# A two-block network on one core: ALiBi bias built on VectorE, norm factors later, q and k of the first group read amid v, and the attentions' value products beside the next scores

## The chip, the cores and the metric

One core of a Trainium2 chip runs the whole program. Its engines run side by side: PE (matmuls; its weight loads are PEld), DVE (VectorE), ACT (ScalarE), POOL (GpSimd) and SP, which issues the DMAs. The metric is the device time of one execution in microseconds (us).

## The reference

The input is a sequence of 256 tokens of width 1024. Two blocks follow each other, each with two layers; all of it is in float32.

```
block 1, layer 0:  h += diff_attention(rmsnorm(h))         8 heads, two softmax maps each
   s = q k^T / 8 - slope[head] * |i - j|                   ALiBi bias
   o = (softmax(s_0) - lam * softmax(s_1)) v ; rmsnorm over each head's 128 ; @ w_o
block 1, layer 1:  h += neighborhood_attention(rmsnorm(h)) 16 heads, windowed bias ; @ w_o
after each of the two:
   h += (silu(n @ w_gate) * (n @ w_up)) @ w_down           n = rmsnorm(h), hidden 2816
   h += sigmoid(rmsnorm(h) @ w_gate_ple) * (p @ w_proj)    "PLE"
h = rmsnorm(h)                                             final norm of block 1
block 2, layer 0:  h += even_mixer(rmsnorm(h))   z = n @ w_in: gated causal convolution | pooling
block 2, layer 1:  h += odd_attention(rmsnorm(h))  8 forgetting heads and 8 block heads, causal
after each of the two: a gated FFN, hidden 2816, with a causal convolution
out = rmsnorm(h)
```

## The kernel before

**Layout.** Activations lie transposed: `h` has the 1024 features on 128 partitions by 8 tiles, and the 256 tokens in the free dimension. A product of weights and activations has 8 steps of k (128 features each). To keep float32 precision on fp32r matmuls each operand is split in a high and a low part, and a product is three matmuls: hi by hi, hi by lo and lo by hi (`mm3`, all at L220). One 128-by-256 output over k = 1024 thus takes 24 matmuls.

**Weights.** SP brings chunks of 512 KB into five stage buffers. `split()` (L96, L97) makes of each chunk `w_hi` on ACT and `w_lo` on DVE, into eight split buffers. Taking a chunk for use triggers the split of a later one, so DVE and ACT have one split to do for every chunk that PE consumes. `W.hold` keeps these splits back while a layer's end is evicted; `release()` and `pay()` let them go, one per tick.

**Order.** PE's order is written by hand. The other engines' orders are made by a scheduler from the program order. `tick()` counts steps: it runs after every 12 matmuls of a weight product. `at(delay, f)` sets a small job `f` (scores, transposes, value products, a norm's factors) at that many ticks later, into the stream of matmuls. The table `AT` has these delays for the three attentions: for two pairs of heads per group, the tick of the scores, and under "then" how long after them the transposes, the values and (da only) the transposes back come. "last" is the group that has no next one.

**Norms.** A norm's gain is multiplied in at once (`norm_bank`: `u_hi` on ACT L282, `u_lo` on DVE L284), its per-token factor later, when products leave PSUM. `stats_bank` sums squares (ACT, DVE L275). `rstd_a` adds the two halves (`half`, DVE L291), sums over partitions with four small matmuls (`ps_ss`), and takes the power -1/2: DVE L306, POOL L307. `rstd_b` spreads the factor with two transposes (`ps_r`, PE L323) and an ACT eviction to `R`. `rstd_soon(n, a, b)` sets `rstd_a` at tick a and `rstd_b` at tick b.

**First products of a layer.** `first_pairs` makes the first two pairs of outputs (four weight chunks) in two passes, so that PE can begin while the last tiles of `u` are still being made: first k = 0 to 5 of all four outputs, then k = 6 and 7. `late=2` is the number of k steps left for the second pass. The banks of `u` (two tiles each) come in order from the layer before.

**Group 0 of an attention** (`qkv_group`) makes the pairs of q and k, then ticks until `R` exists, evicts q and k with it (DVE; ACT L475 and DVE L476 make hi and lo parts), and only then begins v (`ps_v`, 48 matmuls).

**Start.** `small_constants`, at tick 9, makes the ALiBi bias: `dist` on DVE (L571), then eight 128-by-512 `bias` tiles on POOL (L573), the causal masks, and small scalars. POOL takes instructions in order, so the first norm's power at L307 stands behind the eight.

**Block 2, even mixer.** `scale_h` (L932) applies the final norm of block 1 to `h`: eight DVE instructions, at tick 8. The outputs of `w_in` are worked on by DVE alone (`pool_out`, `gc_val` with `z_ev` L972, `gate_b`). In the FFNs `gu` (L835) is the first read of a product, with `R`.

Of the kernel before, what the change touches and what calls it, by code (L numbers as in the profile page):

```python
# [18 lines left out]
S = 256  # L19
# [17 lines left out]
    "da": {"scores": (3, 9), "then": (6, 8, 12), "last": ((2, 5), (5, 7, 10)), 0: (6, 10)},  # L37
    "na": {"scores": (3, 9), "then": (6, 8), "last": ((2, 5), (5, 7)), 0: (6, 10)},
    "od": {"scores": (3, 9), "then": (6, 8), "last": ((2, 5), (5, 7)), 0: (12, 15), 1: (6, 9)},
# [84 lines left out]
def network(ctx: ExitStack, tc: tile.TileContext, x_t, p_t, cols, b_v, na_bias, t5_bias, w_mats, out):  # L124
# [90 lines left out]

    def col(name, i):
        return ct[:, COL[name] + i:COL[name] + i + 1]
# [116 lines left out]
    def rstd_soon(n, a=7, b=9):  # L334
        at(4, release)
        at(a, lambda: rstd_a(n))
        at(b, lambda: rstd_b(n))
# [130 lines left out]
    def qkv_group(n, g, kind, bv, steps):  # L468
# [12 lines left out]
        ps_k = None  # L481
        if g == 0 and kind != "da":
            ps, ps_k = first_pairs(u)
        else:
            ps = pair(u)
            if g == 0:
                ps_k = pair(u)
        while g == 0 and not hasattr(n, "R"):
            tick()
        if kind == "na":  # L490
            t = work.tile([128, 2, S], F32, tag="qb", bufs=1, name="qb")
            nc.vector.tensor_mul(t, ps, bc2(n.R))
            for i in range(2):
                nc.scalar.activation(q[:, i, :], t[:, i, :], AF.Identity, bias=b_q8[:, 2 * g + i:2 * g + i + 1],
                                     scale=0.125)
        else:
            nc.vector.scalar_tensor_tensor(q, ps, 0.125, bc2(n.R), op0=OP.mult, op1=OP.mult)
        q = parts(q, "q")
        ps = ps_k or pair(u)
        if kind == "na":  # L500
            t = work.tile([128, 2, S], F32, tag="qb", bufs=1, name="kb")
            nc.vector.tensor_mul(t, ps, bc2(n.R))
            for i in range(2):
                nc.scalar.activation(k[:, i, :], t[:, i, :], AF.Identity, bias=col("b_k", 2 * g + i), scale=1.0)
        else:
            nc.vector.tensor_mul(k, ps, bc2(n.R))
        k = parts(k, "k")
        steps(q, k, v)
        if kind == "od" and g == 0:
# [3 lines left out]
            for n_k in (3, 3, 2):  # L513
                hi, lo = W.take(n_k * 264)
                for i in range(n_k):
# [5 lines left out]
                    if kk % 2 == 0:  # L521
                        tick()
            for t in range(2):
# [6 lines left out]
        for half in range(2):  # L530
            hi, lo = W.take(1024)
            for i in range(4):
# [5 lines left out]
                if i % 2 == 1:  # L538
                    tick()
        for t in range(2):  # L540
# [29 lines left out]

# [638 lines left out]
```

## Time and profile before

| | |
|---|---|
| median of 3 runs | 1254.99 us (1249.63 to 1255.4) |
| the profiled execution | 1255.7 us, span in the trace 1253.9 us |
| PE busy | 1219.8 us, 97% of the span |
| DVE busy | 930.2 us, 74% |
| ACT busy | 693.4 us, 55% |
| POOL busy | 56.5 us, 5% |
| HBM traffic | 220 MB, 176 GB/s |

A busy share is an average over the whole program. PE does nearly all the time what only PE can do, so what there is to gain or lose lies in three things: the few times at which PE stands still, the clock that it is granted afterwards, and the pace at which equal matmuls follow each other.

### The profile page before, as it was taken

The numbers are of one execution on the slowest core, as the hardware profiler recorded it, in microseconds if no ns is written. First come the engines' busy times: TensorE is split into PE (matmuls) and PEld (weight loads), VectorE is DVE, ScalarE is ACT, GpSimd is POOL, SyncE is SP. The second block draws the span as 40 slices with busy tenths as digits, with TensorE's granted clock in tenths as the row PEclk, the third lists the DMA queues.
The fourth block names the chain that finished last, engine by engine and source line by source line (L and its number), as shares of the span: only waits on it lengthen the run. The fifth ranks groups of instructions, "written<-read, shape, count | busy, mean of one in ns | idle before, by whom it ended". The sixth has DMA issues, their size and how long they took to land.

```text
span 1253.9 us, 25715 instructions
## 1 busy us (share of the span) xinstructions
PE 1219.8 (97%) x10448; PEld 1199.9 (96%) x10448; DVE 930.2 (74%) x1700; ACT 693.4 (55%) x1178; POOL 56.5 (5%) x64
## 2 busy tenths in 40 slices
PE   4999999999999999999999999999999999999997
PEld 4999999999999899999998999999999899999996
DVE  5876766666888767666678978777787876977773
ACT  4776644444667655454457555555455665545543
POOL 6011000000001000000000000000000000000000
PEclk9999999999999999999999999999999999999998
DMA  7554556555557436555544465555545333655530
GB/s 265 186 169 152 174 202 203 196 194 168 202 174 204 175 135 211 193 202 195 180 157 160 160 227 183 200 188 186 185 154 203 122 131 135 218 185 185 187 117 35
DMA packets 62935, 222.46 MB, mean 177 GB/s; under 512 B 7264, under 2 KB 7776, under 8 KB 62688
## 3 DMA queue, kind: packets, MB, share of 16 engines
q1 hardware_dynamic: 60768, 214.52, 50.2%
q0 software_dynamic: 1616, 5.77, 1.9%
q8 instruction: 82, 1.34, 0.4%
q10 hardware_dynamic: 432, 0.53, 0.1%
q14 instruction: 37, 0.30, 0.1%
HBM read 219.74 MB, written 1.05 MB: 176 GB/s over the span
## 4 chain that ended last, share of the span: by engine, by line
PE 86%; DVE 6%; issue 3%; POOL 2%; ACT 2%; DMA 1%; POOLq 0%; DVEq 0%; ACTq 0%; SPq 0%
PE ps_g L220 50%; PE acc L220 26%; PE ps_v L220 4%; DVE w_lo L97 2%; PE ps_V L220 2%; POOL bias L573 1%; PE ps_S L220 1%; PE ps_t L433 1%; POOL rstd L307 1%; ACT w_hi L96 1%; PE ps_p L220 1%; ACT sc L463 0%; PE pz L220 0%; DMA stage<-w_ev_out 0%; PE ps_ss L220 0%
## 5 line engine op out<-in xcount | busy, mean ns | idle before, releaser
L96 ACT ACTIVATE w_hi<-stage 128x1024 fp32r<-128x1024 f32 (+2 forms) x413 | 426.6, 1040 | 411.4 <-PE ps_g L220 174.4
L97 DVE TENSOR_TENSOR w_lo<-stage,w_hi 128x1024 fp32r<-128x1024 f32 (+2 forms) x413 | 493.1, 1201 | 194.8 <-ACT w_hi L96 191.3
L220 PE MATMUL ps_g<-u_hi,w_hi 128*128 128x256 f32 x2048 | 576.5, 281 | 10.2 <-ACT w_hi L96 7.0
L220 PE MATMUL ps_g<-u_hi,w_lo 128*128 128x256 f32 x2048 | 571.1, 279 | 1.2 <-DVE w_lo L97 1.2
L220 PE MATMUL ps_g<-u_lo,w_hi 128*128 128x256 f32 x2048 | 571.3, 279 | 0.7 <-DVE u_lo L284 0.6
L220 PEld LDWEIGHTS ps_g<-u_hi,w_hi 128*128 128x128 f32 x2048 | 386.2, 189 | 14.5 <-ACT w_hi L96 7.0
L220 PEld LDWEIGHTS ps_g<-u_hi,w_lo 128*128 128x128 f32 x2048 | 386.3, 189 | 1.4 <-DVE w_lo L97 1.4
L220 PEld LDWEIGHTS ps_g<-u_lo,w_hi 128*128 128x128 f32 x2048 | 385.8, 188 | 1.1 <-DVE u_lo L284 1.1
L220 PE MATMUL acc<-m,w_hi 128*128 128x256 f32 x1408 | 246.5, 278 | 0.1
L220 PEld LDWEIGHTS acc<-m,w_hi 128*128 128x128 f32 x1408 | 213.6, 188 | 0.4 <-DVE m L805 0.3
L220 PE MATMUL acc<-m,w_lo 128*128 128x256 f32 x704 | 195.4, 278 | 0.0
L220 PEld LDWEIGHTS acc<-m,w_lo 128*128 128x128 f32 x704 | 132.2, 188 | 0.0
L220 PE MATMUL acc<-u_hi,w_hi 128*128 128x256 f32 x256 | 73.0, 285 | 0.0
L220 PE MATMUL acc<-u_hi,w_lo 128*128 128x256 f32 x256 | 71.4, 279 | 0.0
L220 PE MATMUL acc<-u_lo,w_hi 128*128 128x256 f32 x256 | 71.3, 279 | 0.0
L463 ACT ACTIVATE sc<-sc,st 128x256 f32<-128x256 f32 (+1 forms) x96 | 46.0, 481 | 31.4 <-DVE st L461 31.3
L307 POOL TENSOR_TENSOR rstd<-rstd,mhalf 128x2 f32<-128x2 f32 x11 | 15.7, 1426 | 1036.6 <-DVE rstd L306 1036.6
L220 PE MATMUL ps_v<-w_hi,u_hi 128*128 128x256 f32 x176 | 52.5, 298 | 0.0
L220 PE MATMUL ps_v<-w_hi,u_lo 128*128 128x256 f32 x176 | 50.3, 286 | 0.0
L220 PE MATMUL ps_v<-w_lo,u_hi 128*128 128x256 f32 x176 | 50.3, 286 | 0.0
L220 PEld LDWEIGHTS acc<-u_hi,w_hi 128*128 128x128 f32 x256 | 48.0, 188 | 1.5 <-issue 1.1
L220 PEld LDWEIGHTS acc<-u_hi,w_lo 128*128 128x128 f32 x256 | 48.1, 188 | 0.0
(191 smaller groups left out, 1226.8 us busy)
## 6 DMA issues: line engine op xcount, KB each, us to landing
stage<-w_gu SPq DMA_DIRECT2D x88, 512.0 KB, 4.2
stage<-w_in SPq DMA_DIRECT2D x88, 512.0 KB, 4.2
stage<-w_down SPq DMA_DIRECT2D x44, 512.0 KB, 4.3
stage<-w_out SPq DMA_DIRECT2D x44, 512.0 KB, 4.3
stage<-w_na_qkv SPq DMA_DIRECT2D x24, 512.0 KB, 4.2
stage<-w_da_qkv SPq DMA_DIRECT2D x23, 512.0 KB, 4.3
stage<-w_od_in SPq DMA_DIRECT2D x22, 512.0 KB, 3.5
stage<-w_gate SPq DMA_DIRECT2D x16, 512.0 KB, 3.2
```

The costliest lines, as they stand in the source:

```text
L96: self.nc.scalar.activation(hi[:, s], t[:, s], AF.Copy)
L97: self.nc.vector.tensor_sub(lo[:, s], t[:, s], hi[:, s].bitcast(F32))
L220: nc.tensor.matmul(o, a, b, start=start, stop=stop, **kw)
L307: nc.gpsimd.tensor_tensor(n.rstd, st[:, 2:4], mhalf, op=OP.pow)
L433: nc.tensor.transpose(ps[:, o:o + 128], a[:, qt, kk * 128:(kk + 1) * 128], ident)
L463: nc.scalar.activation(sc[:, i, :widths[i]], sc[:, i, :widths[i]], AF.Exp, bias=st[:, 2 + i:3 + i], accum_out=st[:, 4 + i:5 + i])
L573: nc.gpsimd.tensor_scalar(da_tiles[hd // 4][:, hd % 4], dist, -2.0 ** (-8.0 * (hd + 1) / 8), None, op0=OP.mult)
```

## The change

It has five parts. (1) The ALiBi bias moves from POOL to DVE. `dist`, the mask, the pooling counts and three of the eight bias tiles are made at the program's start, the fourth at tick 9 and the other four at tick 22; the second weight chunk is split in two halves. (2) `rstd_soon` spreads a norm's factor one tick later by default (10 for 9). After the FFNs of block 1 both of its steps come two ticks earlier (5 and 7); after the last PLE they are at 7 and 11, with `scale_h` at 13 for 8. (3) Group 0 of an attention no longer ticks until `R` is there: v begins right behind q and k, and q and k are evicted after the first tick of v at which `R` exists; the scores' delays for this group are shorter by one tick (od: two). (4) "then" sets the values at the tick (12) at which the next pair's transposes come, and da's transposes back at 18. (5) `first_pairs` gets `late=4` in na and in the even mixer, and PLE evicts its first two outputs before its third pair of products instead of after.

On DVE, at the program's start, these rows run from the first full-size split to the second split behind `half`, before (`w_lo` is a weight split, `ssq` and `half` are the first norm's sums):

```order
L97 TENSOR_TENSOR w_lo<-stage,w_hi 128x1024
L275 TENSOR_TENSOR ssq<-ssq,sq 128x512
L97 TENSOR_TENSOR w_lo<-stage,w_hi 128x1024 x2
L275 TENSOR_TENSOR ssq<-ssq,sq 128x512
L97 TENSOR_TENSOR w_lo<-stage,w_hi 128x1024
L275 TENSOR_TENSOR ssq<-ssq,sq 128x512
L577 RECIPROCAL rcnt<-rcnt 128x64
L97 TENSOR_TENSOR w_lo<-stage,w_hi 128x1024
L291 TENSOR_TENSOR half<-ssq 128x256
L578 TENSOR_SCALAR off<-off 128x256
L97 TENSOR_TENSOR w_lo<-stage,w_hi 128x1024
L306 TENSOR_SCALAR rstd<-ps_ss 128x2
```

and after, from the last quarter of the first chunk to the same `rstd`:

```order
L97 TENSOR_TENSOR w_lo<-stage,w_hi 128x256
L97 TENSOR_TENSOR w_lo<-stage,w_hi 128x512 x2
L97 TENSOR_TENSOR w_lo<-stage,w_hi 128x1024
L287 TENSOR_TENSOR ssq<-ssq,sq 128x512
L97 TENSOR_TENSOR w_lo<-stage,w_hi 128x1024
L287 TENSOR_TENSOR ssq<-ssq,sq 128x512
L97 TENSOR_TENSOR w_lo<-stage,w_hi 128x1024 x2
L287 TENSOR_TENSOR ssq<-ssq,sq 128x512
L97 TENSOR_TENSOR w_lo<-stage,w_hi 128x1024 x2
L303 TENSOR_TENSOR half<-ssq 128x256
L97 TENSOR_TENSOR w_lo<-stage,w_hi 128x1024
L318 TENSOR_SCALAR rstd<-ps_ss 128x2
```

`half` stood behind five full splits. It now stands behind six, behind the two half-size ones of the second chunk, and, further up, behind three of the `bias` rows. `rstd` follows one split later, as before.

On PE, in the second group of da, at the tick where one pair's scores are made, before (`ps_V` from `ident` are transposes back, `ps_t` transposes, `ps_S` scores, `ps_g` the weight product around them):

```order
L220 MATMUL ps_g<-u_hi,w_lo 128x256
L638 MATMUL ps_V<-ident,on 128x128 x2
L433 MATMUL ps_t<-ident,a 128x128 x4
L220 MATMUL ps_S<-k_hi,q_hi 128x256 x2
L220 MATMUL ps_S<-k_lo,q_hi 128x256 x2
L220 MATMUL ps_S<-k_hi,q_lo 128x256 x2
L220 MATMUL ps_S<-k_hi,q_hi 128x256 x2
L220 MATMUL ps_S<-k_lo,q_hi 128x256 x2
L220 MATMUL ps_S<-k_hi,q_lo 128x256 x2
L220 MATMUL ps_g<-u_hi,w_hi 128x256
```

and after:

```order
L232 MATMUL ps_g<-u_hi,w_lo 128x256
L653 MATMUL ps_V<-ident,on 128x128 x2
L232 MATMUL ps_V<-v,at 128x128 x4
L445 MATMUL ps_t<-ident,a 128x128 x4
L232 MATMUL ps_S<-k_hi,q_hi 128x256 x2
L232 MATMUL ps_S<-k_lo,q_hi 128x256 x2
L232 MATMUL ps_S<-k_hi,q_lo 128x256 x2
L232 MATMUL ps_S<-k_hi,q_hi 128x256 x2
L232 MATMUL ps_S<-k_lo,q_hi 128x256 x2
L232 MATMUL ps_S<-k_hi,q_lo 128x256 x2
L232 MATMUL ps_g<-u_hi,w_hi 128x256
L232 MATMUL ps_g<-u_lo,w_hi 128x256
```

The four value products of the earlier pair (`ps_V<-v,at`), which had their own place two ticks later, now stand in the same break of the weight stream, ahead of the transposes.

On PE at the end of da's last group, before:

```order
L220 MATMUL acc_1426<-u_lo,w_hi 128x256
L220 MATMUL acc_1426<-u_hi,w_lo 128x256
L638 MATMUL ps_V<-ident,on 128x128 x2
L220 MATMUL ps_V<-v,at 128x128 x4
L220 MATMUL acc_1427<-u_hi,w_hi 128x256
L220 MATMUL acc_1427<-u_lo,w_hi 128x256
```

and after:

```order
L232 MATMUL acc_1423<-u_lo,w_hi 128x256
L232 MATMUL acc_1423<-u_hi,w_lo 128x256
L653 MATMUL ps_V<-ident,on 128x128 x2
L232 MATMUL ps_V<-v,at 128x128 x8
L232 MATMUL acc_1424<-u_hi,w_hi 128x256
L232 MATMUL acc_1424<-u_lo,w_hi 128x256
```

Here the transposes back and two pairs' value products fall in one place: ten small matmuls in a row that need three tiles of PSUM tag "m", of which there are two.

```diff
@@ -34,9 +34,9 @@
 
 
 AT = {
-    "da": {"scores": (3, 9), "then": (6, 8, 12), "last": ((2, 5), (5, 7, 10)), 0: (6, 10)},
-    "na": {"scores": (3, 9), "then": (6, 8), "last": ((2, 5), (5, 7)), 0: (6, 10)},
-    "od": {"scores": (3, 9), "then": (6, 8), "last": ((2, 5), (5, 7)), 0: (12, 15), 1: (6, 9)},
+    "da": {"scores": (3, 9), "then": (6, 12, 18), "last": ((2, 5), (5, 7, 10)), 0: (5, 9)},
+    "na": {"scores": (3, 9), "then": (6, 12), "last": ((2, 5), (5, 7)), 0: (5, 9)},
+    "od": {"scores": (3, 9), "then": (6, 12), "last": ((2, 5), (5, 7)), 0: (10, 13), 1: (6, 9)},
 }
 
 
@@ -213,6 +213,18 @@
     causal = off
     tri = const.tile([128, 128], F32, name="tri")
 
+    def da_bias(heads):
+
+        for hd in heads:
+            nc.vector.tensor_scalar(da_tiles[hd // 4][:, hd % 4], dist, -2.0 ** (-8.0 * (hd + 1) / 8), None, op0=OP.mult)
+
+    nc.vector.tensor_scalar(tri, off[:, :128], 0.0, None, op0=OP.is_ge)
+    nc.vector.scalar_tensor_tensor(dist, dist, -1.0, dist, op0=OP.mult, op1=OP.max)
+    da_bias(range(3))
+    for g, w in enumerate(POOL_WINDOWS):
+        nc.vector.tensor_scalar(rcnt[:, g, :], rcnt[:, g, :], float(w), None, op0=OP.min)
+    nc.vector.reciprocal(rcnt, rcnt)
+
     def col(name, i):
         return ct[:, COL[name] + i:COL[name] + i + 1]
 
@@ -331,7 +343,7 @@
     def release():
         W.hold = False
 
-    def rstd_soon(n, a=7, b=9):
+    def rstd_soon(n, a=7, b=10):
         at(4, release)
         at(a, lambda: rstd_a(n))
         at(b, lambda: rstd_b(n))
@@ -478,34 +490,40 @@
 
...
-        ps_k = None
-        if g == 0 and kind != "da":
-            ps, ps_k = first_pairs(u)
+        def evict_q(ps):
...
+            else:
+                nc.vector.scalar_tensor_tensor(q, ps, 0.125, bc2(n.R), op0=OP.mult, op1=OP.mult)
+            return parts(q, "q")
+
+        def evict_k(ps):
...
+            else:
+                nc.vector.tensor_mul(k, ps, bc2(n.R))
+            return parts(k, "k")
+
+        waiting = []
+        if g:
+            qs = evict_q(pair(u))
+            steps(qs, evict_k(pair(u)), v)
         else:
-            ps = pair(u)
-            if g == 0:
-                ps_k = pair(u)
-        while g == 0 and not hasattr(n, "R"):
-            tick()
...
-        ps = ps_k or pair(u)
...
-        k = parts(k, "k")
-        steps(q, k, v)
+            waiting += first_pairs(u, late=4 if kind == "na" else 2) if kind != "da" else [pair(u), pair(u)]
+
+        def read():
+            if waiting and hasattr(n, "R"):
+                qs = evict_q(waiting[0])
+                steps(qs, evict_k(waiting[1]), v)
+                waiting.clear()
+
         if kind == "od" and g == 0:
             z = small.tile([128, 2, 8], F32, tag="zf", bufs=1, name="zf")
             pz = [psum.tile([128, 264], F32, tag=f"acc{2 + t}", name="pz") for t in range(2)]
@@ -520,6 +538,8 @@
                     kk += 1
                     if kk % 2 == 0:
                         tick()
+                        read()
+            assert not waiting
             for t in range(2):
                 nc.scalar.activation(v[:, t, :], pz[t][:, :256], AF.Copy, scale=n.rstd[:, t:t + 1])
                 nc.vector.scalar_tensor_tensor(z[:, t, :], pz[t][:, 256:264], n.rstd[:, t:t + 1],
@@ -537,6 +557,8 @@
                            kk == 0 and t == 0 and c == 0, kk == 7 and c == 2, skip_group_check=True)
                 if i % 2 == 1:
                     tick()
+                    read()
+        assert not waiting
         for t in range(2):
             if kind == "na":
                 nc.vector.scalar_tensor_tensor(v[:, t, :], pv[:, t, :], n.rstd[:, t:t + 1], bv,
@@ -567,14 +589,7 @@
     g_fm = const.tile([128, 8], F32, name="g_fm")
 
     def small_constants():
-
-        nc.vector.scalar_tensor_tensor(dist, dist, -1.0, dist, op0=OP.mult, op1=OP.max)
-        for hd in range(8):
-            nc.gpsimd.tensor_scalar(da_tiles[hd // 4][:, hd % 4], dist, -2.0 ** (-8.0 * (hd + 1) / 8), None, op0=OP.mult)
-        nc.vector.tensor_scalar(tri, off[:, :128], 0.0, None, op0=OP.is_ge)
-        for g, w in enumerate(POOL_WINDOWS):
-            nc.vector.tensor_scalar(rcnt[:, g, :], rcnt[:, g, :], float(w), None, op0=OP.min)
-        nc.vector.reciprocal(rcnt, rcnt)
+        da_bias([3])
         nc.vector.tensor_scalar(causal, off, 128.0, NEG, op0=OP.is_gt, op1=OP.mult)
         l = COL["lam"]
         pr = work.tile([128, 2, 64], F32, tag="dump", bufs=1, name="pr")
@@ -874,12 +889,12 @@
         for b in range(4):
             if b == 0:
                 pgs = first_pairs(n.u, between=proj)
+                continue
+            if b == 1:
                 held = [(i, pps[i], pgs[i]) for i in range(2)]
-            elif b > 1:
+            else:
                 proj(b)
                 held.append((b, pps[b], pair(n.u, *(("m", 2) if b == 2 else ("g", 2)))))
-            if b < 2:
-                continue
             for i, pp, pg in held:
                 z = work.tile([128, 2, S], F32, tag="a", bufs=3, name="z")
                 nc.vector.tensor_mul(z, pg, bc2(n.R))
@@ -899,13 +914,14 @@
 
     n = Norm()
     W.split(4, lambda b: norm_bank(n, b, h[:, 2 * b:2 * b + 2, :], lambda t: col("norm_mix", t)))
-    W.split()
+    W.split(2)
     for b in range(4):
         stats_bank(n, b, h[:, 2 * b:2 * b + 2, :])
         W.split()
     for _ in range(N_HI - 8):
         W.split()
     at(9, small_constants)
+    at(22, lambda: da_bias(range(4, 8)))
     ug = [const.tile([128, 2 + S], F32, name=f"ug{i}") for i in range(3)]
     for t in ug:
         nc.gpsimd.memset(t[:, 0:2], 0.0)
@@ -914,7 +930,7 @@
     for l in range(2):
         n = attention(n, ("da", "na")[l], lambda t, l=l: col("norm_ffn", 8 * l + t))
         n = ffn(n, swiglu_mid, lambda t, l=l: col("norm_ple", 8 * l + t))
-        rstd_soon(n)
+        rstd_soon(n, 5, 7)
         if l == 0:
             def after(nn):
                 rstd_soon(nn)
@@ -932,8 +948,8 @@
             nc.vector.scalar_tensor_tensor(h[:, t, :], h[:, t, :], col("norm_final", t), r,
                                            op0=OP.mult, op1=OP.mult)
 
-    rstd_soon(n)
-    at(8, scale_h)
+    rstd_soon(n, 7, 11)
+    at(13, scale_h)
 
 
     y = split_act()
@@ -1004,7 +1020,7 @@
     plan = [(pool_out, 0), (pool_out, 2), (gc_val, 0), (gc_val, 1), (gate_b, 0), (gc_val, 2), (gc_val, 3), (gate_b, 2)]
     for i, (f, a) in enumerate(plan):
         if i == 0:
-            first = first_pairs(n.u, tags[:2])
+            first = first_pairs(n.u, tags[:2], late=4)
         ps = first[i] if i < 2 else pair(n.u, tags[i], 2 if tags[i] == "g" else 1)
         waiting.append((f, ps, a))
         if hasattr(n, "R"):
```

## Rows read from the trace of the kernel before

**Rows 1.** The page: busy time by engine; the chain that ended last

```profile
PE 1219.8 (97%) x10448; PEld 1199.9 (96%) x10448; DVE 930.2 (74%) x1700; ACT 693.4 (55%) x1178; POOL 56.5 (5%) x64
...
PE 86%; DVE 6%; issue 3%; POOL 2%; ACT 2%; DMA 1%; POOLq 0%; DVEq 0%; ACTq 0%; SPq 0%
```

**Rows 2.** Waits of PE: us in total, times, longest us

```profile
PE ps_r L323 <- POOL rstd L307: 9.0, 4, 7.6
```

**Rows 3.** Timeline of PE, start: start us, us, what, [idle before <- releaser]

```profile
21.31 0.58 PE L220 MATMUL ps_ss<-ones,half 128*128 128x1 f32 x4 [0.51 <-DVE half L291]
...
30.98 0.69 PE L323 MATMUL ps_r<-ident,rstd 128*128 128x128 f32 x2 [7.57 <-POOL rstd L307]
...
38.90 0.28 PE L220 MATMUL ps_g<-u_hi,w_hi 128*128 128x256 f32 x1
```

**Rows 4.** Windows: length, busy (count) by engine, PE clock, DMA share, GB/s

```profile
25.50:35.60 10.10, 4.62 (x22) 4.62 (x23) 3.23 (x5) 3.90 (x7) 5.30 (x5) 0.50 0.19 69
...
104.00:107.30 3.30, 3.30 (x18) 3.30 (x17) 2.11 (x12) 1.83 (x7) 0.00 (x0) 0.50 0.73 266
107.50:675.00 567.50, 564.59 (x4937) 555.97 (x4936) 411.13 (x673) 316.38 (x519) 19.76 (x24) 1.00 0.56 186
677.50:680.70 3.20, 3.20 (x17) 3.20 (x16) 3.15 (x7) 1.17 (x3) 0.00 (x0) 0.50 0.43 152
```

**Rows 5.** Timeline of POOL, first 45 us

```profile
11.73 18.50 POOL L573 TENSOR_SCALAR bias<-dist 128x512 f32<-128x512 f32 x8 [8.93 <-DVE dist L571]
30.20 0.73 POOL L307 TENSOR_TENSOR rstd<-rstd,mhalf 128x2 f32<-128x2 f32 x1
```

**Rows 6.** The chain in order of time, start: start us, us, what

```profile
11.73 10.10 POOL bias L573 x3
...
25.73 1.49 POOL bias L573
```

**Rows 7.** Timeline of DVE, start

```profile
10.95 0.68 DVE L571 SCALAR_TENSOR_TENSOR dist<-dist 128x512 f32<-128x512 f32 x1
...
20.34 0.83 DVE L291 TENSOR_TENSOR half<-ssq 128x256 f32<-128x256 f32 x1
21.09 0.28 DVE L578 TENSOR_SCALAR off<-off 128x256 f32<-128x256 f32 x1
```

**Rows 8.** Timeline of PE, da: the scores that wait for k

```profile
102.18 0.38 PE L220 MATMUL ps_S<-k_hi,q_hi 64*128 64x256 f32 x2 [1.30 <-ACT k_hi L475]
```

**Rows 9.** Timeline of PE: v of na, and a break of it for scores

```profile
429.21 0.28 PE L220 MATMUL ps_v<-w_lo,u_hi 128*128 128x256 f32 x1
429.41 0.39 PE L220 MATMUL ps_S<-k_hi,q_hi 64*128 64x256 f32 x2
```

**Rows 10.** Timeline of DVE, entry of the first FFN

```profile
147.15 4.63 DVE L97 TENSOR_TENSOR w_lo<-stage,w_hi 128x1024 fp32r<-128x1024 f32 x4
151.70 1.28 DVE L835 TENSOR_TENSOR gu<-ps_g,R 128x512 f32<-128x512 f32 x2
```

**Rows 11.** Timeline of PE: entries of na and even mixer; the mixer

```profile
347.52 0.39 PE L220 MATMUL ps_g<-u_hi,w_hi 128*128 128x256 f32 x1 [0.66 <-ACT u_hi L282]
...
675.54 0.38 PE L220 MATMUL ps_g<-u_hi,w_hi 128*128 128x256 f32 x1 [1.87 <-ACT u_hi L282]
676.53 0.38 PE L220 MATMUL ps_g<-u_lo,w_hi 128*128 128x256 f32 x1 [0.61 <-DVE u_lo L284]
...
692.58 0.29 PE L323 MATMUL ps_r<-ident,rstd 128*128 128x128 f32 x1 [1.17 <-DVE rstd L314]
...
721.95 0.39 PE L220 MATMUL ps_g<-u_hi,w_hi 128*128 128x256 f32 x1 [0.70 <-DVE z_ev L972]
```

**Rows 12.** Timeline of DVE: the final norm of block 1

```profile
692.35 2.46 DVE L932 SCALAR_TENSOR_TENSOR h<-h,ct,R 128x256 f32<-128x256 f32 x6
```

**Rows 13.** The chain in order of time: FFNs of both blocks

```profile
165.15 10.88 PE ps_g L220 x96
...
779.42 11.31 PE ps_g L220 x96
```

More of the change, by code (lines that the diff above doesn't have):

```diff
@@ L480, in qkv_group @@
         u = n.u
-        ps_k = None
-        if g == 0 and kind != "da":
-            ps, ps_k = first_pairs(u)
-        else:
-            ps = pair(u)
-            if g == 0:
-                ps_k = pair(u)
-        while g == 0 and not hasattr(n, "R"):
-            tick()
[L490 to L497, printed above, removed]
@@ L498, in qkv_group @@
-        q = parts(q, "q")
-        ps = ps_k or pair(u)
[L500 to L506, printed above, removed]
-        k = parts(k, "k")
-        steps(q, k, v)
+        def evict_q(ps):
+            if kind == "na":
+                t = work.tile([128, 2, S], F32, tag="qb", bufs=1, name="qb")
+                nc.vector.tensor_mul(t, ps, bc2(n.R))
+                for i in range(2):
+                    nc.scalar.activation(q[:, i, :], t[:, i, :], AF.Identity, bias=b_q8[:, 2 * g + i:2 * g + i + 1],
+                                         scale=0.125)
+            else:
+                nc.vector.scalar_tensor_tensor(q, ps, 0.125, bc2(n.R), op0=OP.mult, op1=OP.mult)
+            return parts(q, "q")
@@ new lines, in evict_k @@
+        def evict_k(ps):
+            if kind == "na":
+                t = work.tile([128, 2, S], F32, tag="qb", bufs=1, name="kb")
+                nc.vector.tensor_mul(t, ps, bc2(n.R))
+                for i in range(2):
+                    nc.scalar.activation(k[:, i, :], t[:, i, :], AF.Identity, bias=col("b_k", 2 * g + i), scale=1.0)
+            else:
[5 more added lines that the diff above has]
+            steps(qs, evict_k(pair(u)), v)
+        else:
+            waiting += first_pairs(u, late=4 if kind == "na" else 2) if kind != "da" else [pair(u), pair(u)]
```

## The prediction

> **What bounds the kernel now.** First the busy times: PE is busy for 97% of the span, and 86% of the chain that ended last is PE [rows 1]. So time is to be had only where PE stands still, where its clock is lower afterwards, or where equal matmuls come at a slower pace. Next the waits of PE: the largest that this change can touch is the one for the norms' factors, 9.0 us in four places, 7.6 of them in one [rows 2]. The timeline of PE at the start shows that place: PE stands for 7.57 us before `ps_r`, after 0.51 before `ps_ss`; v ends, and the next products begin, at 38.90 [rows 3]. The windows come third, for the clock. It is granted at 0.50 (1.2 GHz) in the ten microseconds in which that wait ends and half of v runs, and for 3.3 us after two later waits, at 104 and at 677.5; elsewhere it is 1.00 [rows 4]. Such a stretch costs half of itself, about 1.7 us, beyond the wait. Last, the chain in order of time: 96 matmuls take 10.88 us in the FFNs of block 1 and 11.31 in those of block 2, with the same program and clock [rows 13].
>
> **The start.** What holds `ps_r` is POOL: eight bias tiles from 11.73 for 18.50 us, and the power of the first norm (0.73) behind them at 30.20 [rows 5]. All eight leave POOL. In their place DVE gets three of them before `half`. No row shows this operation on DVE. It lies between a one-input operation of half its size, 0.28, and a two-input one of its own size, 0.68 [rows 7]. I take 0.40, nearer to the first, as it too reads one input: 1.2 for the three, 2.0 at most. `half` started at 20.34 and took 0.83 [rows 7], so it ended at 21.17. By the order after it stands behind seven chunks' splits (six whole, one in two halves) instead of five: two more of 1.16 each (4.63 for four) [rows 10] make 2.3, and I add 0.2 for the cut. 21.17 + 1.2 + 2.3 + 0.2 gives 24.9 for `half`, and `ps_ss` starts 0.1 later, as it did before, at 25.0. PE has no more to do before `ps_ss` than it had. Its first wait there, for the last part of the first chunk, grows by about the three tiles (1.2), so it arrives at 20.8 + 1.2 = 22.0 and waits for 3.0, where it waited for 0.5. Behind `ps_ss`: one split on DVE (1.16), the small `rstd`, the power on POOL (0.73) and the hand-overs, 2.8 in all, so 27.8. Meanwhile PE has 12 matmuls and 24 of v to do, 4.2 at full clock, and `ps_r` no longer waits. v ends at 25.0 + 0.5 + 1.4 + 2.8 + 0.4 + 2.8 = 32.9 at full clock. The waits of 7.57, 1.30 and 1.87 [rows 3, 8, 11] each had a fall of the clock behind them [rows 4], the one of 0.66 [rows 11] had none; so I count one fall here, 1.7, and 34.6. That is 6.0 or 4.3 us before 38.90. I take 4.3. The range is 2.5 (tiles at 0.68, one hand-over more) to 9.3 (the whole wait and the clock stretch).
>
> At one place the Trainium skill speaks on this. The row first: three bias tiles on POOL took 10.10 us while DVE was full, and one took 1.49 when it wasn't, while DVE's splits kept their 1.16 [rows 6, 10]. The Trainium skill's page "SBUF — State Buffer" (section "SBUF: two separate sides") says that VectorE and GpSimd share a port pair as an exclusive lock: whichever starts first holds it, and the other fully blocks. By that rule DVE too would have waited for POOL, up to four times 1.49 by 25 us, and would get up to 6 us back, so that v would end near 29; by the rows only POOL paid, and DVE gets nothing back. I go by the rows; the rule's case stands below as a rival.
>
> **da.** The scores of the first pair of a later group wait 1.30 for `k_hi` [rows 8], and the clock falls behind it at 104 [rows 4]. This path (DVE `k`, ACT `k_hi`, DVE `k_lo`, with splits between) is not touched, so both stay. Fewer breaks of the weight stream: a break costs 0.20 instead of 0.12 from start to start (429.21 to 429.41) [rows 9], some 0.09; values now share a break with the next transposes, and I count from PE's order 57 breaks for 66 in the three attentions: -0.8. Against it stands the place at the end of da's last group: three "m" tiles are needed at once where two exist, so the last value products wait until ACT has read the transposes back. An ACT read and a hand-over cost 0.3 to 2.0; I take 0.9. da: +0.2 with its share of the breaks, na and od -0.5.
>
> **Entries of the FFNs.** `R` comes one tick (12 matmuls, 1.4 us) later, and `gu` then stands on DVE behind five splits where it stood behind four, 4.63 [rows 10]. No wait of PE shows there now, so the slack is not known. The price is between 0 and one split (1.16) less what the eight split buffers hold, 0.8. I take 0.25 each, near the lower end since no wait shows: +1.0 for the four.
>
> **na.** Its entry waits 0.66 for `u_hi` [rows 11]. With `late=4` the first pass has 48 matmuls on the first two banks of `u` before it needs a third, and PLE evicts those banks a pair earlier: gone. `ps_r` waited about 0.5 here (the four of rows 2 are 7.6 and three more, 1.4 together): v now lies in front of it: gone. With 0.2 for later scores and 0.4 for breaks: -1.4.
>
> **Even mixer.** Its entry waits 1.87 + 0.61 [rows 11], and the clock falls for 3.3 us behind it [rows 4]: 2.5 + 1.7 = 4.2. With `late=4` the third bank of `u` is needed 36 matmuls (4.2 us) later than before, which covers the 1.87; the last bank is then needed 6 matmuls behind it, and I leave 0.7 of wait for that: -3.5. Bounds: -4.2, and -1.0 if that last bank still costs 1.5 and so the clock. Inside, the wait for the second factor, 1.17 [rows 11], and half a microsecond for the first go. But `scale_h`, 8 instructions of 0.41 (six take 2.46) [rows 12], now stands between the DVE operations that feed `z_ev`, and PE already waits 0.70 for `z_ev` [rows 11]. DVE has the same sum to do up to that point, so what PE gets earlier it waits for there: 0, between -1.7 and +2.
>
> **od.** The fourth `ps_r` wait (0.4) goes, the rest is breaks and the later scores: -1.0 with its share. PLE's factor two ticks earlier: the power's chain (2.8 above at the start, with a full DVE) against 24 matmuls (2.8): no wait, 0.
>
> **Sum.** -4.3 + 0.2 + 1.0 - 1.4 - 3.5 - 1.0 = -9.0. The profiled execution took 1255.7 (span 1253.9), so 1246.7; it stands 0.7 above the median of the runs, so 1246. Its own range takes the distances to the bounds as independent, the root of the sum of their squares: above 1.8 (start), 2.2 (FFN entries), 2.5 and 2 (mixer), 1.1 ("m") make 4.4; below 5.0, 1.0, 0.7, 1.7 and 0.6 make 5.5. So 1241 to 1250.
>
> **Rivals.** *The pace of block 2.* The 96 matmuls at 11.31 instead of 10.88 [rows 13] make 0.43 x 16.5 = 7.1 us for an FFN of 1584 matmuls. The chain has 20 rows of 96 matmuls in block 1's FFNs and 18 in block 2's, each set alike, and between them lies the clock's fall at 677.5 [rows 4]. If the pace is set by such a fall, and the entry of the even mixer no longer causes one, the two FFNs of block 2 keep block 1's: 1246 - 14.2 = 1232, or 1239 for one of them. Against it: no row shows what sets the pace.
>
> *The pace of block 1, the slower side.* The same mechanism the other way. The fall at 104 stays but comes at another place of the stream; if it leaves PE in the slower pace, the FFNs of block 1, from 165 on, take 7.1 more each: 1246 + 14.2 = 1260. It decides from the second FFN on (one alone gives 1253, no change), and with gains under 7.7 instead of 9.0 it is slower than before by over 0.5%. For it: both paces exist at the same clock; against it: block 1's FFNs both came out fast.
>
> *DVE's queue eats the gain.* At the start DVE is full, and the three tiles, two splits and a cut chunk all stand in front of `half`. If the tiles cost 0.68, `half` ends at 26; if the new wait before `ps_ss` then is 4 and v waits for its splits too, the start gives 1.5. With 0.8 for each FFN entry (+3.2), 2.0 for the "m" tiles (da +1.3) and 2 at `z_ev` (mixer -1.5), the sum is -1.5 + 1.3 + 3.2 - 1.4 - 1.5 - 1.0 = -0.9 and the time 1254: no change.
>
> *DVE gets time back.* `half` ends early, no new wait comes before `ps_ss`, and the start gives its full 9.3: 1255 - 9.3 - 4.7 = 1241. For it: three POOL tiles took 10.10 us beside a full DVE [rows 6], so the two do meet; against it: DVE's splits are no longer there than elsewhere. This is what the rule of the Trainium skill named above would make.
>
> **How the numbers follow.** Forecast (1241 to 1250) 0.40; the faster pace in block 2, 0.20; the slower pace in block 1, 0.17; DVE's queue 0.17; DVE gets time back 0.06. A measurement can tell 0.5%, 6.3 us, from no change: faster is below 1248.7, slower above 1261.3. Faster: 0.7 of the forecast (0.28), all of the faster pace (0.20) and of the last (0.06): 0.54 less 0.02 for their tails, 0.52. Slower: the slower pace where gains fall short too (0.08), 0.03 of the queue's upper tail: 0.11. Same: the rest, 0.37. The range leaves out the lower half of the faster pace (0.10) and the part that is slower: 1236 to 1261.
>
> **What would show it.** In the profile after, `ps_r` at the start has no wait and `ps_ss` one of about 3 us; v ends near 34 (29 would speak for the rule, 37 for the queue). Bias rows on DVE are near 0.40. At the even mixer's entry the wait is under 1 and no window at 0.50 follows. The last value products of da wait for "m". The chain's 96 matmuls at 10.88 or 11.31 show by block which pace came out; that the four FFNs are not 10.88, 10.88, 11.31, 11.31 would be what makes the prediction wrong, in either direction.

## The result: slower, and where the time went

The changed kernel takes 1270.5 us (1267.2 to 1274.9, four runs; 1268.1 to 1276.3 in four more) against 1255.2: ratio 1.0133, 95% interval 1.0108 to 1.0159. The forecast was 1246 with a range to 1261, so it was wrong in sign and in range. The profiled execution has a span of 1266.5 us, 12.6 more than before. The page says little: PE is as busy as before in its share [rows 1].

```profile
PE 1233.3 (97%) x10448; PEld 1210.7 (96%) x10448; DVE 932.1 (74%) x1709; ACT 694.0 (55%) x1179; POOL 33.7 (3%) x56
```

The same 10448 matmuls took 13.5 us longer, which neither a wait nor a count explains. PE's waits sum to about what they were; their owners are others [rows 2].

```profile
PE ps_g L232 <- DVE z_ev L988: 3.0, 1, 3.0
PE ps_S L232 <- DVE k_lo L488: 3.0, 4, 1.0
PE ps_g L232 <- ACT u_hi L294: 2.2, 1, 2.2
```

The chain in order of time has the rest. Of each FFN the first row of 96 matmuls [rows 13]:

```profile
160.97 11.31 PE ps_g L232 x96
...
500.81 11.31 PE ps_g L232 x96
...
796.94 10.88 PE ps_g L232 x96
...
1096.95 11.31 PE ps_g L232 x96
```

Block 1's FFNs, at 10.88 before, are at 11.31; the first of block 2 is at 10.88 in this execution, and at 11.31 in another (e4 below). By stage, from one norm's `ps_ss` to the next (those of the PLEs left out, since the change moves them; the last one is 13.7 later than before, and 1.1 comes back behind it):

| stage | change, us |
|---|---|
| start and da | -4.9 |
| FFN 1, PLE 1, entry of na | +7.3 |
| na | +5.8 |
| FFN 2, PLE 2, entry of the mixer | +7.5 |
| even mixer | +2.1 |
| FFN 3 | -6.1 |
| od | +1.4 |
| FFN 4 | +0.6 |

The start did better than forecast. On DVE three bias tiles take 1.09 together, and `half` takes 0.42 [rows 7 had 0.83]:

```profile
10.66 1.09 DVE L219 TENSOR_SCALAR bias<-dist 128x512 f32<-128x512 f32 x3
...
23.14 0.42 DVE L303 TENSOR_TENSOR half<-ssq 128x256 f32<-128x256 f32 x1
```

On PE `ps_ss` and `ps_r` have no wait behind them, and v ends at 31.41 [rows 3: 38.90]. No stretch at half clock follows. PE comes to `ps_ss` just as `half` ends, since its matmuls stand 0.21 apart until 19.2.

```profile
18.95 0.41 PE L232 MATMUL ps_g<-u_hi,w_hi 128*128 128x256 f32 x1
19.16 0.33 PE L232 MATMUL ps_g<-u_lo,w_hi 128*128 128x256 f32 x1
...
23.70 0.58 PE L232 MATMUL ps_ss<-ones,half 128*128 128x1 f32 x4
...
28.46 0.38 PE L335 MATMUL ps_r<-ident,rstd 128*128 128x128 f32 x2
...
31.41 0.28 PE L232 MATMUL ps_g<-u_hi,w_hi 128*128 128x256 f32 x1
```

New waits stand at da's end, in na's last group and in the mixer:

```profile
110.75 0.49 PE L232 MATMUL ps_V<-v,at 128*128 128x128 f32 x2 [1.63 <-DVE u_lo L655]
...
121.99 0.38 PE L232 MATMUL acc<-u_hi,w_hi 128*128 128x256 f32 x1 [0.87 <-ACT u_hi L654]
123.28 0.39 PE L232 MATMUL acc<-u_lo,w_hi 128*128 128x256 f32 x1 [0.91 <-DVE u_lo L655]
...
433.24 0.39 PE L232 MATMUL ps_S<-k_hi,q_hi 64*128 64x256 f32 x2 [1.55 <-ACT k_hi L487]
434.58 0.39 PE L232 MATMUL ps_S<-k_lo,q_hi 64*128 64x256 f32 x2 [0.95 <-DVE k_lo L488]
...
696.58 0.39 PE L232 MATMUL ps_g<-u_hi,w_hi 128*128 128x256 f32 x1 [2.19 <-ACT u_hi L294]
...
738.18 0.38 PE L232 MATMUL ps_g<-u_hi,w_hi 128*128 128x256 f32 x1 [3.03 <-DVE z_ev L988]
```

Behind the waits of na and the mixer the clock falls to 0.50 (columns as in rows 4):

```profile
435.80:439.10 3.30, 3.30 (x17) 2.70 (x18) 1.40 (x8) 1.09 (x4) 0.00 (x0) 0.50 0.35 117
698.60:701.80 3.20, 3.20 (x17) 3.20 (x17) 2.68 (x4) 2.25 (x4) 0.00 (x0) 0.50 0.09 24
739.50:742.70 3.20, 3.20 (x18) 3.20 (x17) 3.20 (x8) 1.05 (x3) 0.00 (x0) 0.50 0.82 264
```

The slower pace begins a few matmuls behind the factor's transposes in the first FFN. First PE, then DVE:

```profile
146.33 0.38 PE L335 MATMUL ps_r<-ident,rstd 128*128 128x128 f32 x2
146.47 0.36 PE L232 MATMUL ps_g<-u_hi,w_hi 128*128 128x256 f32 x1
146.67 0.28 PE L232 MATMUL ps_g<-u_lo,w_hi 128*128 128x256 f32 x1
146.78 0.28 PE L232 MATMUL ps_g<-u_hi,w_lo 128*128 128x256 f32 x1
...
149.16 0.28 PE L232 MATMUL ps_g<-u_hi,w_lo 128*128 128x256 f32 x1
149.39 0.39 PE L232 MATMUL ps_g<-u_hi,w_hi 128*128 128x256 f32 x1
149.62 0.28 PE L232 MATMUL ps_g<-u_lo,w_hi 128*128 128x256 f32 x1
149.73 0.28 PE L232 MATMUL ps_g<-u_hi,w_lo 128*128 128x256 f32 x1
149.85 0.28 PE L232 MATMUL ps_g<-u_hi,w_hi 128*128 128x256 f32 x1
```

```profile
142.26 4.63 DVE L97 TENSOR_TENSOR w_lo<-stage,w_hi 128x1024 fp32r<-128x1024 f32 x4
147.51 1.23 DVE L97 TENSOR_TENSOR w_lo<-stage,w_hi 128x1024 fp32r<-128x1024 f32 x1 [0.61 <-ACT w_hi L96]
148.65 1.28 DVE L850 TENSOR_TENSOR gu<-ps_g,R 128x512 f32<-128x512 f32 x2
```

The matmuls start every 0.113 until 149.16. There PE stops for about 0.1 us, as `gu`, behind a fifth split (four before [rows 10]), frees the next PSUM tile; the matmul behind the stop takes 0.1 longer too. From 149.62 on they start every 0.118, for 1523 matmuls. The stop costs 0.2, the pace behind it 7. The runs below test whether it is the stop.

### The profile page after: what moved, and what is told of

Read it like the earlier page. It is cut to its first block, busy times and chain, and to the rows that moved or that the text cites. A ratio compares the mean times of both kernels' runs of the same rounds, so it can differ in the third digit from the quotient of the medians.

```text
span 1266.5 us, 25716 instructions
## 1 busy us (share of the span) xinstructions
PE 1233.3 (97%) x10448; PEld 1210.7 (96%) x10448; DVE 932.1 (74%) x1709; ACT 694.0 (55%) x1179; POOL 33.7 (3%) x56
## 4 chain that ended last, share of the span: by engine, by line
PE 79%; DVE 7%; ACT 2%; issue 1%; DMA 0%; POOLq 0%; DVEq 0%; ACTq 0%; SPq 0%
PE ps_g L232 47%; PE acc L232 25%; PE ps_v L232 3%; DVE w_lo L97 2%; PE ps_V L232 1%; PE ps_t L445 1%; ACT w_hi L96 1%; PE ps_S L232 1%; PE pz L232 0%; DVE u_lo L296 0%; PE ps_p L232 0%; DVE h L905 0%; DVE z L900 0%; DMA stage<-w_ev_out 0%; PE ps_ss L232 0%
## 5 line engine op out<-in xcount | busy, mean ns | idle before, releaser
L232 PEld LDWEIGHTS acc<-u_lo,w_hi 128*128 128x128 f32 x256 | 48.1, 188 | 1.1 <-DVE u_lo L655 1.1
```

Source lines behind the costliest of these rows:

```text
L232: nc.tensor.matmul(o, a, b, start=start, stop=stop, **kw)
```

## The experiments

Times are compared with runs of the kernel before on the same chip (medians from 1254.2 to 1255.3). Paces are us per 96 matmuls, read in the chain, of the four FFNs in order.

**e1 and e2: the one tick.** e1 is the kernel after, e2 the kernel before, each with only the factor's tick changed at the FFNs' entries.

```diff
-        rstd_soon(nn)          # e1: at the ends of the attentions and of the even mixer
+        rstd_soon(nn, 7, 9)
-        rstd_soon(nn)          # e2: the same places in the kernel before
+        rstd_soon(nn, 7, 10)
```

> The kernel after, with the norm's factor spread at tick 9 instead of 10 at the four entries of the FFNs and nowhere else. Theory A (the later factor makes PE stop for 0.1 us inside the first FFN products, and the pace in which it starts again then holds for the whole FFN): the stop is gone from the trace, the two FFNs of block 1 go back from 11.31 to 10.88 us per 96 matmuls as before the change, and the time falls by about 14 us, to 1254 to 1258. Theory B (the pace of an FFN is drawn anew in every execution, whatever the kernel): the stop is gone but the FFNs come out at either pace, and the median stays at 1264 to 1273. Theory C (pace has nothing to do with breaks of the stream): the paces are as in the kernel after, 11.31, 11.31, 10.88, 11.31.

> The kernel before, with the factor at tick 10 instead of 9 at the four entries of the FFNs and nowhere else. Theory A: a stop of PE of 0.1 us appears behind the factor's transposes, the FFNs of block 1 go to 11.31 us per 96 matmuls, and the time rises by about 14 us, to 1268 to 1271. Theory B: the stop appears, the paces are mixed, and the time lies within 7 us of before. Theory C: paces as before, 10.88, 10.88, 11.31, 11.31, and a time of 1255 to 1257.

e1: 1260.6 us (1256.7 to 1263.9 in six runs; ratio to before 1.0049, 1.0025 to 1.0074), paces 10.88, 10.88, 11.31, 11.31; the stop is gone, and DVE reaches `gu` behind four splits. e2: 1269.0 (1.0112, 1.0096 to 1.0129), all four at 11.31, with the stop at 153.12. Theory A holds in both for the paces; e1's time is above the 1254 to 1258 that it gave, as other losses stay (e5). So one tick at four places costs 13.7 us in the kernel before and 12.5 (1273.1 to 1260.6) in the kernel after. The first FFN of e1, then of e2:

```profile
160.47 10.88 PE ps_g L232 x96
```

```profile
164.69 11.31 PE ps_g L220 x96
```

**e3 and e4: both kernels again**, unchanged.

> The kernel before, unchanged, for a second profiled execution. Theory A: each FFN has the pace that it had in the first profile (10.88, 10.88, 11.31, 11.31) and the span is within 2 us of 1253.9. Theory B: at least one FFN has the other pace, and the spans differ by multiples of about 7 us.

> The kernel after, unchanged, for a second profiled execution. Theory A: paces 11.31, 11.31, 10.88, 11.31 again, with a span near 1266.5. Theory B: another mixture of paces, and a span that differs by multiples of about 7 us (the four runs so far, 1267.2 to 1274.9, lie 7.7 apart at most).

e3: 1255.4, the chain's rows at the paces of the first profile. They hide a difference in FFN 3. Between the factor's transposes and the first output product (`acc`) lie 83 matmuls. In the first profile they start every 0.118:

```profile
763.83 0.28 PE L220 MATMUL ps_g<-u_lo,w_hi 128*128 128x256 f32 x1
...
773.49 0.28 PE L220 MATMUL ps_g<-u_hi,w_lo 128*128 128x256 f32 x1
```

In e3, the same program, they start every 0.113. PE then reaches `acc` before DVE's `m` is done, stops, and goes on at 0.118:

```profile
764.33 0.28 PE L220 MATMUL ps_g<-u_lo,w_hi 128*128 128x256 f32 x1
...
773.62 0.28 PE L220 MATMUL ps_g<-u_hi,w_lo 128*128 128x256 f32 x1
773.73 0.73 PE L220 MATMUL acc<-m,w_hi 128*128 128x256 f32 x2
774.31 0.28 PE L220 MATMUL acc<-m,w_lo 128*128 128x256 f32 x1
```

```profile
773.61 0.75 DVE L805 TENSOR_TENSOR m<-t,m 128x256 fp32r<-128x256 f32 x2
```

e7, e9 and e10 below show the same in FFN 3. e4: 1273.1, all four at 11.31. FFN 3 has the other pace, and has it already in the 22 matmuls ahead of the stop (113 ns in the first profile of this kernel, 118 in e4). So theory A holds for FFNs 1, 2 and 4, and theory B for FFN 3: there the pace behind the factor's transposes, a break of PE's own order, differs between executions of one program. The eight runs of the kernel after lie in two groups, three at 1267 to 1268 and five at 1273 to 1276, as such an FFN would give; that the pace of FFN 3 parts them was not shown run by run.

**e11: a break without a wait**, in the kernel before.

```diff
+        def turn():
+            ps = psum.tile([128, 128], F32, tag="m", bufs=2, name="ps_x")
+            nc.tensor.transpose(ps, ident, ident)
+        if kind != "od":
+            at(12, turn)
```

> The kernel before with one more 128 by 128 transpose on PE, whose result nobody reads, three ticks behind the factor's transposes in the FFNs of block 1 and in the first FFN of block 2: a break of the weight stream at about the place of the stop that the late factor causes, without any wait. Theory A1 (any break at that place redraws the pace): at least one of block 1's FFNs goes to 11.31 us per 96 matmuls, the time rises by 7 or 14 us. Theory A2 (only a restart after a wait is slow): both stay at 10.88, time within 1 us of before.

It was put in block 1's two FFNs alone, not in block 2's as the text says. 1267.7 (1.0114, 1.0095 to 1.0132), all four at 11.31: A1 holds, and a wait isn't needed. One transpose, with no idle time ahead of it, costs 7 us in each of two FFNs:

```profile
151.55 0.28 PE L220 MATMUL ps_g<-u_hi,w_lo 128*128 128x256 f32 x1
151.67 0.27 PE L738 MATMUL ps_x<-ident 128*128 128x128 f32 x1
151.70 0.36 PE L220 MATMUL ps_g<-u_hi,w_hi 128*128 128x256 f32 x1
151.90 0.28 PE L220 MATMUL ps_g<-u_lo,w_hi 128*128 128x256 f32 x1
...
163.25 11.31 PE ps_g L220 x96
```

**e5: values early again**, on top of e1.

```diff
-    "da": ... "then": (6, 12, 18),   "na", "od": ... "then": (6, 12)
+    "da": ... "then": (6, 8, 12),    "na", "od": ... "then": (6, 8)
```

> The kernel after with the factor at tick 9 at the FFNs' entries (as e1), and with the table's "then" as before the change: values at 8, da's transposes back at 12. Compared with e1 (1260.6 us, span 1258.0). Theory A (the values that share a tick with the next transposes and scores come so late that da's and na's last groups stall): the waits of e1 at da's end (1.62, 0.87, 0.91), of na's last group for k (1.55 and 0.96, with a clock fall of 3.4 us behind them) and for the last values (0.74, in od 0.63) go, and the time falls by 6 to 9 us, to 1252 to 1255. Theory B (the waits for k come from q and k read amid v): the k waits and the clock fall stay, only the 3.4 + 1.4 of the value waits go, less 0.8 for nine breaks more: 1256 to 1258.

1249.6 (1243.1 to 1250.7 in five runs; 0.9945, 0.9921 to 0.9969), 10.9 below e1; theory A holds, with more than it said. The waits at da's end and for the last values are gone, and in na's last group the scores start without the 1.55; na takes 117.3 us, where it took 123.5 in e1 and 116.8 before:

```profile
423.38 0.39 PE L232 MATMUL ps_S<-k_hi,q_hi 64*128 64x256 f32 x2
```

Why values that come four ticks later delay `k` in na wasn't separated: DVE's and ACT's queues both shift.

**e6 and e7: the mixer's entry and its scaling**, each on top of e1.

```diff
-        for ks in (range(KT - late), range(KT - late, KT)):           # e6
+        for ks in (range(4), range(4, 6), range(6, 8)):               # where late is 4
-    rstd_soon(n, 7, 11)                                               # e7
-    at(13, scale_h)
+    rstd_soon(n, 7, 9)
+    at(8, scale_h)
```

> The kernel e1, with the first pairs of na and of the even mixer in three passes (k 0 to 3, then 4 and 5, then 6 and 7) instead of two (0 to 3, 4 to 7). Theory A (with late=4 the last bank of u is asked for 6 matmuls behind the third, where it was 60 behind before, so PE waits for the last bank): the entry waits of e1 (0.47 and 0.60 in na, 3.02 in the mixer, with a clock fall) shrink to under 1 in all, 3 to 4 us less than e1. Theory B (DVE's queue is the limit; PE gets the same data at the same time and waits as long, at another place): the sum of waits until the first norm's sums of the mixer stays within 1 us of e1's 4.1 and so does the time.

> The kernel e1, with the even mixer's norm as before the change: both factors' spreads and the scaling of h at ticks 9 and 8. Theory A (scaling h in front of the second z_ev makes PE wait there): the wait for z_ev falls from 2.6 to under 1, waits of 0.5 and 1.2 for the factors return, the time is within 1 us of e1's. Theory B (the scaling costs the mixer more than it gives, since a clock fall follows the longer wait): the time falls by 1.5 to 3 us.

e6: 1260.0 (ten runs from 1254.0 to 1267.4), the same as e1. The entry wait shrinks from 3.02 to 0.98, and 3.02 appears before the norm's sums: theory B, DVE finishes the last bank of `u` no sooner, whatever PE does ahead of it.

```profile
681.76 0.39 PE L232 MATMUL ps_g<-u_hi,w_hi 128*128 128x256 f32 x1 [0.98 <-ACT u_hi L294]
...
687.55 0.37 PE L232 MATMUL ps_ss<-ones,half 128*128 128x1 f32 x1 [3.02 <-DVE half L303]
```

e7: 1259.1, ten runs from 1254.5 to 1265.8, 1.5 below e1 but within the two intervals (1.0018 to 1.0063; e1 1.0025 to 1.0074). The `z_ev` wait falls from 2.60 to 1.08. Unclear in time.

**e8: another place for block 2's breaks**, in the kernel before.

```diff
-        rstd_soon(nn)               # behind od
+        rstd_soon(nn, 6, 9)
-    rstd_soon(n)                    # behind the even mixer
+    rstd_soon(n, 6, 8)
```

> The kernel before, with the places of the norm's steps at the entries of block 2's FFNs moved: at the first, sums at tick 6 and factor at 8 (7 and 9 before), at the second, sums at 6 and factor at 9. No new wait of PE is expected. Theory A (the pace in which PE starts again behind a break depends on the place of that break in its stream): at least the first of the two FFNs changes from 11.31 to 10.88 us per 96 matmuls, and the time falls by about 7 or 14 us. Theory B (block 2's FFNs are at 11.31 for a reason of their own): both stay at 11.31 and the time within 1 us of 1255.

Both stay at 11.31 (theory B). The time, 1249.7 (0.9966, 0.9949 to 0.9982), is lower all the same, and why isn't shown. In its profile the clock doesn't fall at da's scores, far ahead of the edit, but that execution took 1253.6, more than the median. Of the kernel before, too, single runs are at 1249 to 1251.

**e9 and e10: what to keep.** e9 is the kernel before with the bias on DVE, part (1) of the change, and nothing else. e10 is e5 with the mixer and PLE as before the change.

```diff
+    da_bias(range(3))                      # e9, on the kernel before: with dist, at the start
-            nc.gpsimd.tensor_scalar(da_tiles[hd // 4][:, hd % 4], dist, ...)
+        da_bias([3])
-    W.split()
+    W.split(2)
+    at(22, lambda: da_bias(range(4, 8)))
-            first = first_pairs(n.u, tags[:2], late=4)       # e10, on e5; PLE's loop and
+            first = first_pairs(n.u, tags[:2])               # scale_h (as e7) as before, too
```

> The kernel before with the first part of the change alone: the bias on DVE, three tiles at the program's start, the second chunk in halves. v still waits for the factor in group 0. Theory A (POOL's eight tiles were what held the first factor): the wait of 7.6 us before the factor's transposes falls to 2 to 3, behind a wait of 1 to 2.5 for half, no long stretch at half clock remains, and the first FFN's sums come 4 to 6 us earlier than before (146.5): time 1249 to 1251. Theory B (DVE's longer queue gives it back, and v in front of the transposes is what wins the time): under 3 us, 1252 to 1255.

> The change without the parts that lost: e5 (factor at tick 9 at the FFNs, values early) and the even mixer and PLE as before the change (late=2, both factors and the scaling of h at 9 and 8, the first two outputs of PLE evicted behind the third pair). Kept are the bias on DVE, q and k read amid v, late=4 in na, and the earlier factor in PLE. Theory A (the mixer's entry wait of 3.0 with a clock fall and the z_ev wait of 2.3 with another came from these parts): waits there sum to 4 to 5 with one clock fall less, and the time is 2 to 4 us below e5's 1249.6. Theory B (the waits move but their sum stays): within 1 us of e5.

e9: 1247.4 (0.9945, 0.9931 to 0.9958); e10: 1247.3 (twelve runs from 1242.6 to 1256.8; 0.9946, 0.9929 to 0.9963). Part (1) alone gives 7.5 us, more than theory A said: `ps_r` doesn't wait at all, though v stands behind it, and v ends within 0.3 us of the kernel after's.

```profile
25.80 0.43 PE L334 MATMUL ps_r<-ident,rstd 128*128 128x128 f32 x2
...
31.72 0.28 PE L231 MATMUL ps_g<-u_hi,w_hi 128*128 128x256 f32 x1
```

The parts that e10 adds to it give nothing together: reading q and k amid v, `late=4` in na, and PLE's earlier factor. In the mixer e10's waits fall from e5's 5.6 us to 4.3, with one clock fall less, as its theory A said; the times don't tell its theories apart (ratio 0.9946, e5 0.9945).

**e12 to e15: which break leads to which pace**, on e9: `n` transposes in one place per FFN, at these ticks. Each of the four is a single run.

```diff
+    def pause(n):
+        ps = psum.tile([128, 512], F32, tag="m", bufs=2, name="ps_x")
+        for i in range(n):
+            nc.tensor.transpose(ps[:, i * 128:(i + 1) * 128], ident, ident)
+        at(tick, lambda: pause(n))
```

> The kernel e9 (bias on DVE alone) with two more 128 by 128 transposes on PE, read by nobody, at tick 12 of each of the four FFNs: twelve ticks behind the sums' start, three behind the factor's transposes. In e11 one such transpose at this place sent both FFNs of block 1 to 11.31 (e11 had it in these two FFNs alone). Theory K (the kind of break decides: the factor's two transposes left a fast pace in block 1, one transpose a slow one): two transposes here leave block 1 at 10.88. Theory P (the place in the stream decides, whatever breaks it there): block 1 goes to 11.31 as in e11. Theory Q (block 2's FFNs are slow for a reason of their own): both stay at 11.31.

> The kernel e9 with one more transpose, at tick 13 in the FFN behind da and in the one behind the even mixer, at tick 14 in the other two. Theory K: all four at 11.31. Theory P: ticks 13 and 14 are new places, and at least one of the four has the pace other than at tick 12 (block 1 at 10.88, or block 2 at 10.88). Theory Q: block 2 stays at 11.31 in both.

> The kernel e9 with two more transposes, at ticks 13, 14, 15 and 16 of the four FFNs in their order. Theory K: block 1 at 10.88 in both. Theory P: the same pace as with one transpose at the same tick (13 in the first FFN and 14 in the second, as in e13). Theory Q: block 2 at 11.31.

> The kernel e9 with four more transposes at tick 12 in the first and the last FFN, and three in the other two. Theory K: four (even) as with two, three (odd) as with one. Theory P: paces as in e12 whatever the number. Theory Q: block 2 at 11.31.

| | FFN 1 | FFN 2 | FFN 3 | FFN 4 | us |
|---|---|---|---|---|---|
| e9, none | 10.88 | 10.88 | 11.31 | 11.31 | 1247.4 |
| e12, two at 12 | 11.31 | 11.31 | 11.31 | 10.88 | 1254.2 |
| e13, one at 13, 14, 13, 14 | 11.31 | 11.31 | 11.31 | 11.31 | 1259.6 |
| e14, two at 13, 14, 15, 16 | 11.31 | 11.31 | 11.31 | 10.88 | 1256.7 |
| e15, four, three, three, four at 12 | 11.31 | 11.31 | 11.31 | 11.31 | 1262.2 |

Each theory fails somewhere: K at FFN 1 in e12, P at FFN 4 in e12 and e15 (same place, other pace), Q at FFN 4. Every extra break in block 1 loses the fast pace; FFN 4 gains it behind two transposes, and behind one or four it doesn't.

**e16 and e17: a break that helps**, on e9.

```diff
+        if kind == "od":
+            at(12, lambda: pause(2))       # e16 and e17
+    at(12, lambda: pause(2))               # e17, behind the even mixer
+    at(13, lambda: pause(2))
```

> The kernel e9 with two more transposes, read by nobody, at tick 12 of the last FFN alone. Theory P (the pace behind a break is fixed by the program around it and comes out alike in every execution): the last FFN is at 10.88 us per 96 matmuls as in e12, the others as in e9 (10.88, 10.88, 11.31), and the median is 6 to 7 us under e9's 1247.4: 1240 to 1242. Theory R (the fast pace in e12 and e14 was drawn by chance): the runs fall in two groups 7 us apart, or all stay at 1247.

> As e16, with two breaks of two transposes each, at ticks 12 and 13, in the FFN behind the even mixer. One such break left that FFN at 11.31 (e12, e14). Theory S (a break exchanges the two paces or leaves them by the place): a second one has a chance of about one in three to reach 10.88, and then the time is 1233 to 1235. Theory Q (that FFN is slow for a reason of its own): it stays at 11.31, 1240 to 1242.

e16: 1240.6 (0.9884, 0.9869 to 0.9900), four runs from 1239.5 to 1241.3: theory P for FFN 4, whose break works in every run, and this kernel beats both. FFNs 1 to 3 are at 10.88, 10.88 and 11.31 as in e9; FFN 4:

```profile
1074.50 10.88 PE ps_g L231 x96
```

e17: 1240.5, the same; FFN 3's rows stay at 11.31, the time of theory Q. But a reason of FFN 3's own isn't what the trace shows. The first of the two breaks leads to the fast pace, for 11 matmuls 0.113 apart, and the second ends it, an exchange at each break as in theory S:

```profile
759.89 0.28 PE L231 MATMUL ps_g<-u_lo,w_hi 128*128 128x256 f32 x1
...
761.02 0.28 PE L231 MATMUL ps_g<-u_hi,w_lo 128*128 128x256 f32 x1
761.14 0.38 PE L353 MATMUL ps_x<-ident 128*128 128x128 f32 x2
```

## Why the prediction was wrong

- *Entries of the FFNs* (+0.25 each): the step that failed. The order was read rightly (`gu` behind five splits), and the stop it causes costs 0.2 us, as was taken. What it missed is that such a break can change the pace of the whole stretch behind it: the stages of block 1's two FFNs took 7.3 and 7.5 us longer, and with one tick back (e1) 12.5 us of the loss go.
- *The pace rivals* had the size (7.1 for an FFN, up to 14.2 for two) and the wrong cause: they hung it on falls of the clock. In e3 and e9 a fall at da's scores and one at the mixer stand where they stood, in e8 the first is missing, and the chain's rows have the same paces in all three; in e11 one transpose alters them.
- *The start* (-4.3, measured -7.5 at v's end): the bias tiles cost 0.36 instead of 0.40, `half` ends at 23.6 instead of 24.9, and no clock fall follows. The forecast had PE wait 3.0 for `half`; PE itself came 1.7 later than said, since its matmuls ran at half pace until 19.2. With the same start e1 and e7 wait 0.92 and 2.49 there and begin `ps_ss` at 23.6 and 23.7, so `half` sets this time, as forecast. What the rivals called DVE's time back is seen in a few short rows with POOL idle: `half` at 0.42 instead of 0.83, and two `pr` rows at 0.36 instead of 0.69. There the trace agrees with the Trainium skill, page "SBUF — State Buffer", section "SBUF: two separate sides", by which one of the two engines holds the shared port pair for a whole instruction and the other blocks. The splits, also two-input operations, show nothing of it (1.22 for one at 16.25, and 1.21 at 12.44 before, beside POOL's tiles).
- *da* (+0.2, measured +2.6): the parts as written, 0.9 for the tile less the 0.3 that na and od leave of the 0.8 for breaks, make +0.6. The last value products wait 1.63 for a PSUM tile where 0.9 was taken, and two further waits of 0.9 follow, as the last heads' outputs come late for the output product. `k`'s wait of 1.30 and its clock fall [rows 8, 4], said to stay, went in this kernel and came back in e5.
- *na* (-1.4, measured +5.8): the later values were counted as nine breaks saved; e5 shows that they cost na the waits for `k` and a clock fall (6.2 us from e1 to e5).
- *Even mixer* (entry -3.5, inside 0): the entry gave nothing and the inside cost 2.1. `late=4` moved PE's need of the third bank later, as said, and that of the last bank from matmul 72 to matmul 54, which the forecast didn't count; moved back to 72 in e6, the wait only goes elsewhere: DVE's end of PLE is the limit. The `z_ev` wait grew to the 3.0 that the upper bound (+2) allowed, and a clock fall came with it.
- *od* (-1.0, measured +1.4): only 0.4 of the forecast has a row. Part (4) again: od takes 117.5 us in e1 and 115.5 in e5, 116.1 before.

What stays open: what makes the pace behind a given break 113 or 118 ns, why it differs from execution to execution in FFN 3, and why later values delay `k` in na. Where FFN 3 takes the fast pace in a kernel with the factor at tick 9 (e3, e7, e9, e10), PE meets DVE's `m` too early, and that stop ends it.

## What to carry to other kernels

Before a long uniform stretch of matmuls, compare the time of equal rows of the chain between stages; where two values exist, look at the last break ahead of the stretch, and cost every edit that adds or moves a break there at the whole stretch, not at the break. Look at the rows directly behind the break too, as a later stop can hide what it did (FFN 3 of e3). If only one part of a large change has a wait that ends the chain behind it (here POOL's eight tiles), try that part alone first: here it gave all that the change had to give (e9 against e10).

## What was not expected of the hardware

- Equal fp32r matmuls with the same granted clock run at one of two paces, 113.3 or 117.8 ns from start to start, and keep it for as long as nothing breaks the stream (1583 matmuls in one run). A break of 0.1 us, a wait or a transpose, can exchange them. In FFNs 1 and 2 the factor's transposes were followed by the fast pace in all 19 profiles, and any later break by the slow one. In FFN 3 the pace behind the same transposes was not the same in two executions of one program, for the kernel before and for the kernel after.
- Two useless transposes made a kernel 6.8 us faster (e9 to e16).
